# Score products of 128 columns, a doubled key rest, split compressed keys and separate pools for small tiles in a two-layer attention trunk

## The chip, the cores and the metric

The kernel runs on one core of one Trainium2 chip. The metric is device time in microseconds (us) of one execution; lower is better. The engines named below are PE (TensorE: matrix products and the loads of their stationary operand, shown apart as PEld), DVE (VectorE), ACT (ScalarE), POOL (GpSimd) and SP (SyncE, which here only issues DMA transfers).

## The reference

A sequence of 1024 tokens of width 1024 goes through two decoder layers in float32. Layer 0 has sparse attention with three branches, layer 1 has dilated sliding-window attention, and each is followed by a SwiGLU. There are 16 heads of width 64 in 4 groups (`g`), and the 4 heads of a group share keys and values. Cut to what the change touches:

```
def nsa_attention(h, ...):                      # layer 0
    q, kc, vc, ks, vs, kwn, vwn, gl = split(h @ w_in)
    k_cmp = gelu(blocks(kc) @ w1) @ w2          # 63 compressed keys per group
    s = q @ k_cmp.T * dh**-0.5 + bias           # (1) compressed branch
    p_cmp = softmax(s)
    imp = sum_heads(p_cmp) @ overlap            # importance of 16 blocks of 64 keys
    sel = top_k(imp + forced, 8)                # 8 of 16 blocks per query and group
    o_sel = softmax(q @ ks.T + bias, keys of sel)  @ vs     # (2) selected blocks, causal
    o_win = softmax(q @ kwn.T + bias, 0 <= i - j <= 255) @ vwn   # (3) window
    return (g0 * o_cmp + g1 * o_sel + g2 * o_win) @ w_out

def dilated_attention(h, ...):                  # layer 1: three (window, dilation) groups,
    for window, dilation in ((128, 1), (512, 4), (2048, 16)):    # merged by their denominators
        o, lse = banded attention over every dilation-th key
```

## The kernel before

Activations lie transposed, so that heads stand on partitions. To keep float32 accuracy with the fast product type, an operand is split into a high part and a rest (`split`: ACT writes the high part, DVE the difference). A query tile `Q` holds the high part of 64 dimensions in partitions 0 to 63 and its rest in partitions 64 to 127. A key tile whose high part (or rest) is stored twice, in both halves of the partitions (`load_k` does that with two DMAs), therefore gives the product with the whole query in one pass. A score is the sum of two products: query times key high part (first line, L676) and query times key rest (second line, L677).

**Layer 0's attention** (called A here) works on 32 units, `(g, t)`: 4 groups by 8 blocks of 128 queries. `jobs` yields for each unit two window jobs (`dense_job` with `br` 2, one for each pair of heads `hp`), the compressed job of the next unit (`cmp_job`) and two jobs over the selected keys (`dense_job` with `br` 1). Block `t` sees the keys of blocks 0 to `t`, so a selected job has `n = 128 * (t + 1)` columns. From `t` = 4 on, the choice of blocks is applied in the product itself: the second product takes its query from `QM`, with 16 mask rows below the 64 rows of the high part, and the key rest with the block indicator `bS` in rows 64 to 79, 80 rows in all. For `t` below 4 all blocks are chosen; there the second product uses the 64 rows of the key rest alone. A job's scores go through a fused add-bias-and-minimum on DVE (L679), exp on ACT (L685), the scaling by 1/sum and gate on POOL (L689), and then, in `back` and two jobs later, through PE transposes (L276), a split on ACT (L139) and DVE (L140), and the products with the values (L297 to L299).

Products narrower than 256 columns are done 256 wide before the change, as in `w, rw = max(hi - lo, 256), hi - lo`, and the surplus columns are never read. The compressed scores (L601) take the 64-column key tile `kc` in plain float32; the built program has 128 such products, and the profile shows two hardware instructions for each.

**Layer 1's attention** (called B) has for each group eight `wide_job` positions `r` (dilation 4, L1490, and dilation 16, L1495, side by side in one bank) and eight `near_job` positions `t` (dilation 1, L1510), two jobs each. `unit` does for them what `dense_job` does (DVE L1454, ACT L1459). `load_first` loads the first group's operands in three pieces, since their producers finish just before. The row minima and sums go into the small tiles `st12` and `st0`.

**What sets the order.** The order on each engine's queue is set when the program is built, by a scheduler that runs the traced program through a timing model of its own; each engine then executes its queue strictly in order. Tiles come from pools, which are laid on two stacks of on-chip memory. A new pool may lie on memory that an earlier stage still uses; the first instruction that writes a tile there waits for the last users of the old one. DMAs with `nc.sync` are all in SP's one queue, those with `nc.gpsimd` in POOL's. Before the change, the small tiles of a few columns (`m`, `sm`, `cm`, `st12` and others) are in the same pool `wk` as the large ones. In A, the key rest and all else that does not fit earlier lies in pool `aB` (`kB`), which comes after the projections.

Of the kernel before, what the change touches and what calls it, by code (L numbers as in the profile page):

```python
# [24 lines left out]
G = 4  # L25
# [66 lines left out]
def trunk(ctx, tc, I, out):  # L92
# [244 lines left out]
    kc = ares.tile([128, G, DH], F32, name="kc")  # L337
# [5 lines left out]
    with ExitStack() as c:  # L343
# [51 lines left out]
        def compress(i, kc2, weights):  # L395
            pe, w1, w2 = (("a_pe_k", "a_w1_k", "a_w2_k"), ("a_pe_v", "a_w1_v", "a_w2_v"))[i]
            pet = cp.tile([128, 16], F32, name="pet", bufs=2)
            nc.gpsimd.dma_start(pet, I[pe][0].rearrange("(i two) d -> (two d) i", two=2))
            w2t = cp.tile([128, 2, 2, 64], F32, name="w2t", bufs=1)
            for u in range(2):  # L400
                nc.gpsimd.dma_start(w2t[:, :, u, :], I[w2][0].rearrange("(a p) d -> p a d", p=128))
            ps = [bank(f"cmp{hd}")[:, :256] for hd in range(2)]
            for q in range(4):
                wh, wl = weights.load(I[w1][0][q * 512:(q + 1) * 512, :], 4, 256)
                for r in range(4):
                    ch = 4 * q + r
# [12 lines left out]
            yield  # L419
            ps2 = bank("cmp0")[:, :256]  # L420
            if i == 0:
                hh = cp.tile([128, 2, 256], F32R, name="hh")
                hl = cp.tile([128, 2, 256], F32R, name="hl")
                split(hh, hl, hid)
                w2h = cp.tile([128, 2, 128], F32R, name="w2h")
                w2l = cp.tile([128, 2, 128], F32R, name="w2l")
                split(w2h, w2l, w2t[:].rearrange("p a u d -> p a (u d)"))
                for hd in range(2):
                    mm3(ps2, (w2h[:, hd], w2l[:, hd]), (hh[:, hd], hl[:, hd]), hd == 0, hd == 1)
                nc.vector.tensor_copy(kc, ps2.rearrange("p (g n) -> p g n", n=DH))  # L430
# [87 lines left out]
    with ExitStack() as c:  # L518
# [11 lines left out]
        rC = Ring("C", [128, 4, 63], F32, [(kA1, 1), (kB, 1)])  # L530

        rM = Ring("QM", [128, 4, 512], F32R, [(kB, 1)])
        force = kB.tile([128, NT, 16], F32, name="force")
        nc.sync.dma_start(force, I["force"])
        crow = kB.tile([128, 1], F32, name="crow")
# [12 lines left out]
        def load_bias(g, a, heads=range(4)):  # L548
# [4 lines left out]
            for hh in heads:  # L553
# [3 lines left out]
                if a == 1:  # L557
# [4 lines left out]
                    nc.gpsimd.tensor_copy(C[:, hh, 31:], every)  # L562
# [4 lines left out]
        def load_ks(g):  # L567
            K = grp["K", g] = [rKs.tile() for _ in range(2)]
            load_k(K[0], kS[0, g, 0])
            nc.sync.dma_start(f32(K[1][0:64]), kS[0, g, 1])  # L570
            nc.sync.dma_start(f32(K[1][64:80]), bS)

# [21 lines left out]
        def cmp_job(g, t):  # L594
# [3 lines left out]
            for hp in range(2):  # L598
                ps = bank("s")[:].rearrange("p (e n) -> p e n", e=2)
                for e in range(2):  # L600
                    nc.tensor.matmul(ps[:, e, :DH], f32(query(g, t, 2 * hp + e)), kc[:, g, :], start=True, stop=True)  # L601
                    psv.append(ps[:, e, :])
# [3 lines left out]
            mx = wk.tile([128, 4], F32, name="cm", bufs=3)  # L606
            dn = wk.tile([128, 4], F32, name="cd", bufs=3)
# [11 lines left out]
            dg = wk.tile([128, 4], F32, name="dg", bufs=3)  # L619
            nc.vector.tensor_mul(dg, dn, gt(g, t, 0, 0, 4))  # L620
            if t >= 4:
                pn = wk.tile([128, 4, 64], F32, name="pn", bufs=2)
                nc.gpsimd.tensor_mul(pn[:, :, :nv], pv, dn[:].unsqueeze(2).to_broadcast([128, 4, nv]))
            nc.gpsimd.tensor_mul(pv, pv, dg[:].unsqueeze(2).to_broadcast([128, 4, nv]))
            if t >= 4:
                a4 = wk.tile([128, 68], F32, name="a4", bufs=2)
# [3 lines left out]
                sc = wk.tile([128, 16], F32, name="sc", bufs=2)  # L630
# [3 lines left out]
                m8 = wk.tile([128, 8], F32, name="m8", bufs=2)  # L634
                nc.vector.max(out=m8, in_=sc)
                s2_ = wk.tile([128, 16], F32, name="s2", bufs=2)
                nc.vector.match_replace(out=s2_, in_to_replace=m8, in_values=sc, imm_value=-3e38)
                mk = wk.tile([128, 16], F32, name="mk", bufs=2)
# [13 lines left out]
        def dense_job(g, t, br, hp):  # L652
# [5 lines left out]
            mm = wk.tile([128, 2], F32, name="m", bufs=8)  # L658
            sm = wk.tile([128, 2], F32, name="sm", bufs=8)
            masked = br == 1 and t >= 4  # L660
            kh, kl = grp["K", g] if br == 1 else grp["KW", g, t // 4]
            skip = 256 if br == 2 and t >= 4 else 0
            cuts = [(0, n - 512, 0), (n - 512, n, 1)] if n > 512 else [(0, n, 1)]
            mp = wk.tile([128, 2, 2], F32, name="mp", bufs=4) if len(cuts) == 2 else None
            for e in range(2):
                hh = 2 * hp + e
                q = query(g, t, hh)
                for i, (lo, hi, a) in enumerate(cuts):
                    bias = grp["T", g, a, hh] if br == 1 else grp["TW", g, hh]
                    ps = bank("s")  # L670
                    w, rw = max(hi - lo, 256), hi - lo
                    ks = slice(k0 * 128 - skip + lo, k0 * 128 - skip + lo + w)

                    nr = 128 if br == 2 else 80 if masked else 64
# [34 lines left out]
        def jobs():  # L709
# [4 lines left out]
            load_ks(0)  # L714
            load_v(0, 0, 0)
            yield lambda: cmp_job(*units[0])
            for i, u in enumerate(units):
# [7 lines left out]
                elif g + 1 < G:  # L725
# [4 lines left out]
                    elif t == 4:  # L730
                        load_q(g + 1, 0)
                    elif t == 6:
# [640 lines left out]
    with ExitStack() as c:  # L1373
        wk = pool(c, "bw")
        bB = pool(c, "bB")
        c.push(open_banks(("s",), ("pt",), ("o",)))
# [15 lines left out]
        def load_first():  # L1392
# [4 lines left out]
            for lo, hi in ((0, 256), (256, 512), (512, 1024)):  # L1397
                for i in (1, 2):
# [5 lines left out]
                    ks = slice(2 * lo, 2 * hi) if i == 1 else slice(lo + 128 * (lo > 0), min(hi + 128, S))  # L1404
# [78 lines left out]
        def wide_job(g, r, hp):  # L1483
            (Q1, K1, V1), (Q2, K2, V2) = grp[1, g], grp[2, g]

            def score(ps, hh):
# [5 lines left out]
                w = min(256, S - r * 128)  # L1492
                with after(prev):
                    for z in range(2):
                        nc.tensor.matmul(ps[:, 256:256 + w], Q2[hh][:, qs], K2[z][:, r * 128:r * 128 + w],  # L1495
                                         start=z == 0, stop=z == 1)
# [6 lines left out]
        def near_job(g, t, hp):  # L1503
# [4 lines left out]
            def score(ps, hh):  # L1508
                for z in range(2):
                    nc.tensor.matmul(ps[:, :256], Q0[hh][:, t * 128:(t + 1) * 128],  # L1510
                                     K0[z][:, k0 * 128:k0 * 128 + 256], start=z == 0, stop=z == 1)
# [5 lines left out]
        def merge(g):  # L1517
# [14 lines left out]
            s12 = wk.tile([128, NT, 8], F32, name="s12", bufs=2)  # L1532
# [3 lines left out]
            for hf in range(2):  # L1536
                yield
                cc = wk.tile([128, 4, 8], F32, name="cc", bufs=2)
                mx = wk.tile([128, 4, 4], F32, name="mx", bufs=2)
# [35 lines left out]
        def jobs():  # L1575
# [9 lines left out]
            for g in range(G):  # L1585
                grp["st", g] = (wk.tile([128, NT, 8], F32, name="st12", bufs=2),
                                wk.tile([128, NT, 8], F32, name="st0", bufs=2),
# [77 lines left out]
```

## Time and profile before

| | |
|---|---|
| runs before | 3013.38, 3020.68, 3022.80 us; median 3020.68 us |
| profiled execution | 3014.07 us |
| its span, first to last instruction | 3012.3 us (1.8 us lie around it) |
| mean granted PE clock | 0.984 |
| busy share of the span | PE 95%, PEld 79%, DVE 80%, ACT 53%, POOL 54% |
| A, first compressed score (L601) to last value product (L299) | 286.57 to 746.00 us |
| B, first wide score (L1490) to last product with the values merged (L1571) | 1910.24 to 2230.39 us |

The three runs differ by 0.3%. The profiled execution is 6.6 us below their median. In the profile's rows a name such as `s<-K,Q` is the tile written and the tiles read, with buffer numbers left out; `64*128 64x256` is a product whose stationary operand has 64 rows and 128 columns and whose moving operand has 64 rows and 256 columns. The times of matrix products overlap, because their ends are modelled: the pace of PE is read from the distance of starts, and best from the starts of the weight loads.

### The profile page before, as it was taken

What the parts mean: (1) busy time and instruction counts of PE and PEld (TensorE: products, weight loads), DVE (VectorE), ACT (ScalarE), POOL (GpSimd) and SP (SyncE); (2) the same over time, 40 slices, a digit from 0 to 9 for tenths busy, and PEclk for the clock granted to TensorE, in tenths of its full rate; (3) what the DMA queues carried; (4) which work ended last, traced back from release to release, by engine and by line L of the source; (5) the groups of instructions that cost most, each with busy time, mean ns of one, the idle gap of its engine ahead of it and who ended that gap; (6) DMA issues with size and microseconds to landing.
All of it is one profiled execution on the core that took longest, in us unless ns stands there. A gap on an engine that the chain in (4) does not pass through costs nothing.

```text
span 3012.3 us, 44147 instructions
## 1 busy us (share of the span) xinstructions
PE 2869.0 (95%) x14670; PEld 2378.2 (79%) x14670; DVE 2405.6 (80%) x4832; ACT 1600.7 (53%) x3596; POOL 1640.1 (54%) x1751
## 2 busy tenths in 40 slices
PE   7999999999889999999999999899988999999997
PEld 6988888888667878888777788788866778888886
DVE  4432888988988898898875677588899788889887
ACT  5432888887363333333364444689964533333334
POOL 2134666666766555555556787333347655555551
PEclk9999999999999999999999999999999999999999
DMA  6765032121212223222124555866520212111111
GB/s 171 221 193 167 24 105 79 33 60 58 73 51 65 64 63 78 67 58 72 56 94 143 157 164 149 267 199 183 147 95 25 63 49 63 53 53 57 56 46 74
DMA packets 266196, 293.43 MB, mean 97 GB/s; under 512 B 17971, under 2 KB 209347, under 8 KB 265968
## 3 DMA queue, kind: packets, MB, share of 16 engines
q1 hardware_dynamic: 246320, 230.45, 26.6%
q0 software_dynamic: 19648, 60.16, 6.6%
q8 instruction: 116, 1.90, 0.3%
q14 instruction: 112, 0.92, 0.1%
HBM read 227.44 MB, written 78.81 MB: 102 GB/s over the span
## 4 chain that ended last, share of the span: by engine, by line
PE 61%; DVE 22%; ACT 6%; issue 5%; DMA 3%; POOL 2%; SPq 1%; DVEq 0%; ACTq 0%; POOLq 0%
DVE pl L763 7%; PE ux L166 5%; DVE xr L821 5%; PE ux L167 5%; PE ux L168 4%; PE pt L276 4%; PE uy L166 4%; PE uy L167 4%; PE uy L168 4%; PE dx L167 3%; PE mm L166 3%; PE dx L168 3%; PE mm L167 3%; PE mm L168 2%; PE dr L166 2%
## 5 line engine op out<-in xcount | busy, mean ns | idle before, releaser
L763 DVE TENSOR_TENSOR pl<-oT,ph 128x512 fp32r<-128x512 f32 x315 | 333.7, 1079 | 40.8 <-ACT ph L762 34.6
L762 ACT ACTIVATE ph<-oT 128x512 fp32r<-128x512 f32 x329 | 198.8, 626 | 222.3 <-PE ux L167 58.5
L276 PE MATMUL pt<-ident,P 128*128 128x128 f32 x1536 | 244.5, 278 | 10.9 <-ACT P L1459 2.7
L763 DVE TENSOR_TENSOR pl<-oTb,ph 128x512 fp32r<-128x512 f32 x229 | 228.1, 1021 | 24.0 <-ACT ph L762 23.9
L762 ACT ACTIVATE ph<-oTb 128x512 fp32r<-128x512 f32 x239 | 143.1, 625 | 185.4 <-PE ux L167 51.4
L821 DVE TENSOR_TENSOR xr<-xr,dr 128x512 f32<-128x512 f32 x336 | 214.4, 678 | 28.2 <-PE dr L168 28.1
L140 DVE TENSOR_TENSOR tl<-pt,th 128x512 fp32r<-128x512 f32 (+1 forms) x320 | 206.9, 651 | 30.8 <-ACT th L139 28.7
L821 DVE TENSOR_TENSOR xr<-xr,dx 128x512 f32<-128x512 f32 x352 | 220.1, 676 | 2.9 <-PE dx L168 2.2
L167 PE MATMUL dx<-pl,ph 128*128 128x512 f32 x512 | 203.2, 401 | 9.7 <-DVE pl L763 8.6
L689 POOL TENSOR_SCALAR P<-P,sm,gates 128x384 f32<-128x384 f32 (+7 forms) x256 | 182.5, 724 | 54.1 <-DVE sm L687 48.2
L276 PEld LDWEIGHTS pt<-ident,P 128*128 128x128 f32 x1536 | 179.6, 142 | 29.9 <-ACT P L1459 6.7
L168 PE MATMUL dx<-ph,pl 128*128 128x512 f32 x512 | 199.9, 397 | 0.3 <-DVE pl L763 0.3
L139 ACT ACTIVATE th<-pt 128x512 fp32r<-128x512 f32 (+1 forms) x320 | 176.8, 563 | 41.1 <-PE pt L276 35.2
L685 ACT ACTIVATE P<-P,m 128x384 f32<-128x384 f32 (+7 forms) x256 | 170.8, 669 | 16.2 <-DVE m L683 8.2
L1082 POOL TENSOR_TENSOR oT<-oT,gffn 128x512 f32<-128x512 f32 x92 | 108.2, 1183 | 128.7 <-DMA oT<-in_ffn_w_up_dram 112.4
L166 PE MATMUL dx<-ph 128*128 128x512 f32 x512 | 157.3, 398 | 8.4 <-DVE xr L821 3.3
L1082 POOL TENSOR_TENSOR oTb<-oTb,gffn 128x512 f32<-128x512 f32 x92 | 106.1, 1160 | 92.6 <-DMA oTb<-in_ffn_w_up_dram 83.1
L299 PE MATMUL o<-tl,V 128*128 128x256 f32 x540 | 147.6, 298 | 8.4 <-POOL tl L292 4.4
L298 PE MATMUL o<-th,V 128*128 128x256 f32 x540 | 149.6, 294 | 2.4 <-ACT th L139 1.3
L291 POOL TENSOR_SCALAR th<-traw 128x128 fp32r<-128x128 f32 (+1 forms) x112 | 74.8, 671 | 126.9 <-ACT traw L290 46.3
L1459 ACT ACTIVATE P<-P,st 128x384 f32<-128x384 f32 (+2 forms) x256 | 139.5, 547 | 7.7 <-PE pt L1570 4.1
L167 PEld LDWEIGHTS dx<-pl,ph 128*128 128x128 f32 x512 | 97.5, 190 | 40.7 <-DVE pl L763 21.1
(617 smaller groups left out, 9547.6 us busy)
## 6 DMA issues: line engine op xcount, KB each, us to landing
qB<-xr POOLq DMA_DIRECT2D x96, 256.0 KB, 4.9
oT<-in_ffn_w_up_dram SPq DMA_DIRECT2D x92, 256.0 KB, 3.0
oTb<-in_ffn_w_up_dram SPq DMA_DIRECT2D x92, 256.0 KB, 3.0
Q<-qB SPq DMA_DIRECT2D x40, 512.0 KB, 8.2
wd<-in_ffn_w_down_dram SPq DMA_DIRECT2D x66, 256.0 KB, 2.7
oT<-in_b_w_q_dram SPq DMA_DIRECT2D x48, 256.0 KB, 3.4
K<-kBs SPq DMA_DIRECT2D x40, 256.0 KB, 10.3
wraw<-in_a_w_in_dram SPq DMA_DIRECT2D x18, 512.0 KB, 5.0
```

What stands on the lines that cost most here:

```text
L139: nc.scalar.activation(H_, src, AF.Copy)
L140: nc.vector.tensor_sub(L_, src, f32(H_))
L166: nc.tensor.matmul(ps, lh, rh, start=first, stop=False, skip_group_check=bool(shared))
L167: nc.tensor.matmul(ps, lh, rl, start=False, stop=False, skip_group_check=bool(shared))
L168: return nc.tensor.matmul(ps, ll, rh, start=False, stop=last, skip_group_check=bool(shared))
L276: nc.tensor.transpose(ps[:, i * 128:(i + 1) * 128], b, ident)
L685: nc.scalar.activation(P[:, e, :n], P[:, e, :n], AF.Exp, bias=mm[:, e:e + 1], scale=-1.0, accum_out=sm[:, e:e + 1])
L689: nc.gpsimd.tensor_scalar(P[:, e, :n], P[:, e, :n], sm[:, e:e + 1], gt(g, t, br, 2 * hp + e, 1), op0=OP.mult, op1=OP.mult)
L762: nc.scalar.activation(h, src, AF.Copy)
L763: (eng or nc.vector).tensor_sub(l, src, f32(h))
L821: nc.vector.tensor_add(xs, xs, banks[t])
L1082: nc.gpsimd.tensor_mul(v, v, gains[:, k:k + 4].unsqueeze(2).to_broadcast([128, 4, 128]))
```

## The change

Five edits, all in the two attentions:

- Score products are as wide as their scores: 128 columns where 256 were computed. In the built program 352 products become 128 wide: 96 in A, 256 in B (224 of `wide_job`'s dilation 16, 32 of `near_job` at `t` = 0).
- For `t` below 4, the second selected product no longer uses 64 rows: a new tile `KD` of 512 columns holds the key rest in both halves of the partitions, loaded by `load_kd` with two DMAs per group, and the product has 128 rows. There are 64 of these products. The mathematical sum gains the small product of both rests.
- The compressed keys are split into two tiles (`kch`, `kcl`), and each of the 128 products becomes two of the fast type.
- Small tiles move into pools of their own (`as` in A, `bs` in B), opened after the large ones, `crow` among them; `pn` has one buffer instead of two; `C` is 64 wide.
- `load_first` loads the dilation-16 keys in pieces of 256, 256 and 512 columns instead of 384, 256 and 384.

```diff
-    kc = ares.tile([128, G, DH], F32, name="kc")
+    kc = [ares.tile([128, G, DH], F32R, name=f"kc{z}") for z in "hl"]
...
-                nc.vector.tensor_copy(kc, ps2.rearrange("p (g n) -> p g n", n=DH))
+                split(*kc, ps2.rearrange("p (g n) -> p g n", n=DH))
...
-        rC = Ring("C", [128, 4, 63], F32, [(kA1, 1), (kB, 1)])
-
+        rC = Ring("C", [128, 4, 64], F32, [(kA1, 1), (kB, 1)])
+
+        rKd = Ring("KD", half, F32R, [(kB, 1)])
...
-        crow = kB.tile([128, 1], F32, name="crow")
+        ws = pool(c, "as")
+        crow = ws.tile([128, 1], F32, name="crow")
...
+        def load_kd(g):
+            t = grp["KD", g] = rKd.tile()
+            load_k(t, kS[0, g, 1][:, 0:512])
...
-                    nc.tensor.matmul(ps[:, e, :DH], f32(query(g, t, 2 * hp + e)), kc[:, g, :], start=True, stop=True)
+                    for z in range(2):
+                        nc.tensor.matmul(ps[:, e, :DH], query(g, t, 2 * hp + e), kc[z][:, g, :], start=z == 0,
+                                         stop=z == 1)
...
-                pn = wk.tile([128, 4, 64], F32, name="pn", bufs=2)
+                pn = wk.tile([128, 4, 64], F32, name="pn", bufs=1)
...
-            mm = wk.tile([128, 2], F32, name="m", bufs=8)
-            sm = wk.tile([128, 2], F32, name="sm", bufs=8)
+            mm = ws.tile([128, 2], F32, name="m", bufs=8)
+            sm = ws.tile([128, 2], F32, name="sm", bufs=8)
             masked = br == 1 and t >= 4
             kh, kl = grp["K", g] if br == 1 else grp["KW", g, t // 4]
+            if br == 1 and not masked:
+                kl = grp["KD", g]
...
-                    w, rw = max(hi - lo, 256), hi - lo
+                    w = rw = hi - lo
...
-                    nr = 128 if br == 2 else 80 if masked else 64
+                    nr = 80 if masked else 128
...
             load_ks(0)
+            load_kd(0)
...
                         load_q(g + 1, 0)
+                        load_kd(g + 1)
...
+        ws = pool(c, "bs")
...
-                    ks = slice(2 * lo, 2 * hi) if i == 1 else slice(lo + 128 * (lo > 0), min(hi + 128, S))
+                    ks = slice(2 * lo, 2 * hi) if i == 1 else slice(lo, hi)
...
-                w = min(256, S - r * 128)
                 with after(prev):
                     for z in range(2):
-                        nc.tensor.matmul(ps[:, 256:256 + w], Q2[hh][:, qs], K2[z][:, r * 128:r * 128 + w],
-                                         start=z == 0, stop=z == 1)
+                        nc.tensor.matmul(ps[:, 256:384], Q2[hh][:, qs], K2[z][:, qs], start=z == 0, stop=z == 1)
...
-                    nc.tensor.matmul(ps[:, :256], Q0[hh][:, t * 128:(t + 1) * 128],
-                                     K0[z][:, k0 * 128:k0 * 128 + 256], start=z == 0, stop=z == 1)
+                    nc.tensor.matmul(ps[:, :n], Q0[hh][:, t * 128:(t + 1) * 128],
+                                     K0[z][:, k0 * 128:k0 * 128 + n], start=z == 0, stop=z == 1)
...
-                grp["st", g] = (wk.tile([128, NT, 8], F32, name="st12", bufs=2),
-                                wk.tile([128, NT, 8], F32, name="st0", bufs=2),
+                grp["st", g] = (ws.tile([128, NT, 8], F32, name="st12", bufs=2),
+                                ws.tile([128, NT, 8], F32, name="st0", bufs=2),
                                 wk.tile([128, 2, S], F32, name="o12", bufs=2))
```

The edit changes the scheduler's input, and the order of A and B differs in many places; outside them it does not differ but for a few rows. Three places matter below. The first is PE's queue in A, third group, `t` = 2. `K_4608` and `K_4609` are the key's high part and rest, `VW` and `KW` belong to the window. Before:

```order
L648 MATMUL o<-th,vc 128x512
L649 MATMUL o<-tl,vc 128x512
L298 MATMUL o<-th,V_4614 128x256
L676 MATMUL s<-K_4608,Q_5145 128x384
L677 MATMUL s<-K_4609,Q_5145 128x384
L676 MATMUL s<-K_4608,Q_5147 128x384
L677 MATMUL s<-K_4609,Q_5147 128x384
L299 MATMUL o<-tl,V_4614 128x256
```

After:

```order
L297 MATMUL o<-traw,VW_5721 128x256
L276 MATMUL pt<-ident,P_6553 128x128 x4
L686 MATMUL s<-K_4659,Q_5208 128x384
L687 MATMUL s<-KD_5212,Q_5208 128x384
L298 MATMUL o<-th,V_4665 128x256
L686 MATMUL s<-K_4659,Q_5210 128x384
L687 MATMUL s<-KD_5212,Q_5210 128x384
L299 MATMUL o<-tl,V_4665 128x256
```

The pairs of score products stand as they did, close together among value products; the second of a pair now reads `KD`.

The second place is SP's queue where A's last loads before its first unit stand, with the waits that the built program gives them (DMAHW is an earlier DMA on a queue of SP, DMASW one of POOL). Before:

```order
L581 DMA V_2601<-vS 128x4x128 [waits DMAHW4_49]
L534 DMA force<-in_force_dram 128x128 [waits DMAHW5_49]
L536 DMA crow<-in_cmprow_dram 128x1 [waits DMAHW6_49]
L546 DMA QM_2585<-qS 64x4x512 [waits DMAHW7_49]
L555 DMA T_2729<-sA 128x512 [waits DMAHW0_49]
```

After:

```order
L587 DMA V_2613<-vS 128x4x128 [waits DMAHW4_49]
L538 DMA crow<-in_cmprow_dram 128x1 [waits DMAHW5_49,PE_49]
L535 DMA force<-in_force_dram 128x128 [waits DMAHW6_49]
L268 DMA KD_2551<-kS 64x512 [waits DMAHW7_49]
L269 DMA KD_2551<-kS 64x512 [waits DMAHW0_49]
L548 DMA QM_2597<-qS 64x4x512 [waits DMAHW1_49]
```

`crow` now stands first and waits for PE: its new place is memory that holds the projections' last operand `hH7` until then. `force`, both loads of `KD` and `QM` stand behind it.

The third place is DVE's queue at the start of B, where the last results of the projections (`xr`, which POOL's DMAs store to `qB`) are followed by the first scores. Before:

```order
L1022 TENSOR_TENSOR c_19386<-c_19386,dr1_19357 128x512 [waits Activation_49]
L143 SCALAR_TENSOR_TENSOR xr_9957<-uy_19248,xr_9957 128x512 [waits Activation_49]
L1038 TENSOR_TENSOR d1_19351<-d1_19351,dr1_19357 128x512 [waits PE_49]
L143 SCALAR_TENSOR_TENSOR xr_9957<-d1_19351,xr_9957 128x512 [waits Activation_49]
L1454 ISA P_19567,st12_19564<-s_19568,T120_19477 128x384 [waits DMAHW4_49,DMAHW3_49,PE_49]
L1454 ISA st12_19564 128x1
```

After:

```order
L1050 TENSOR_TENSOR d1_19497<-d1_19497,dr1_19503 128x512 [waits PE_49]
L143 SCALAR_TENSOR_TENSOR xr_10103<-d1_19497,xr_10103 128x512 [waits Activation_49]
L1394 CAST rowsel_19620<-rows_19618 128x512 [waits DMAHW3_49]
L1467 ISA P_19716,st12_19713<-s_19717,T120_19626 128x384 [waits DMASW4_49,DMASW3_49,DMASW5_49,DMASW2_49,DMASW6_49,DMASW1_49,DMASW7_49,DMASW0_49,DMAHW4_49,DVE_49,PE_49]
L1467 ISA st12_19713 128x1
```

The first score instruction now waits for POOL's DMAs too, since pool `bs` lies on the end of `xr`.

More of the change, by code (lines that the diff above doesn't have):

```diff
@@ L561, in load_bias @@
                     grp["TW", g, hh] = w_
-                    nc.gpsimd.tensor_copy(C[:, hh, 31:], every)
+                    nc.gpsimd.tensor_copy(C[:, hh, 31:63], every)
                 else:
@@ L605, in cmp_job @@
             nc.gpsimd.memset(pc[:, :, nv:64], 0.0)
-            mx = wk.tile([128, 4], F32, name="cm", bufs=3)
-            dn = wk.tile([128, 4], F32, name="cd", bufs=3)
+            mx = ws.tile([128, 4], F32, name="cm", bufs=3)
+            dn = ws.tile([128, 4], F32, name="cd", bufs=3)
             for hh in range(4):
@@ L618, in cmp_job @@
                 nc.vector.tensor_scalar(dn, dn, crow, None, op0=OP.mult)
-            dg = wk.tile([128, 4], F32, name="dg", bufs=3)
+            dg = ws.tile([128, 4], F32, name="dg", bufs=3)
             nc.vector.tensor_mul(dg, dn, gt(g, t, 0, 0, 4))
             if t >= 4:
-                pn = wk.tile([128, 4, 64], F32, name="pn", bufs=2)
+                pn = wk.tile([128, 4, 64], F32, name="pn", bufs=1)
                 nc.gpsimd.tensor_mul(pn[:, :, :nv], pv, dn[:].unsqueeze(2).to_broadcast([128, 4, nv]))
@@ L625, in cmp_job @@
             if t >= 4:
-                a4 = wk.tile([128, 68], F32, name="a4", bufs=2)
+                a4 = ws.tile([128, 68], F32, name="a4", bufs=2)
                 nc.gpsimd.memset(a4, 0.0)
@@ L629, in cmp_job @@
                                         op=OP.add)
-                sc = wk.tile([128, 16], F32, name="sc", bufs=2)
+                sc = ws.tile([128, 16], F32, name="sc", bufs=2)
                 nc.vector.tensor_reduce(sc, a4[:, 1:65].rearrange("p (j i) -> p j i", i=4), axis=AX.X, op=OP.add)
@@ L633, in cmp_job @@
                 nc.vector.tensor_add(sc, sc, force[:, t, :])
-                m8 = wk.tile([128, 8], F32, name="m8", bufs=2)
+                m8 = ws.tile([128, 8], F32, name="m8", bufs=2)
                 nc.vector.max(out=m8, in_=sc)
-                s2_ = wk.tile([128, 16], F32, name="s2", bufs=2)
+                s2_ = ws.tile([128, 16], F32, name="s2", bufs=2)
                 nc.vector.match_replace(out=s2_, in_to_replace=m8, in_values=sc, imm_value=-3e38)
-                mk = wk.tile([128, 16], F32, name="mk", bufs=2)
+                mk = ws.tile([128, 16], F32, name="mk", bufs=2)
                 nc.vector.tensor_scalar(mk, s2_, -2e38, BIG, op0=OP.is_gt, op1=OP.mult)
@@ L657, in dense_job @@
             P = wk.tile([128, 2, 1024 if br == 1 else 384], F32, name=f"P{br}", bufs=4)
-            mm = wk.tile([128, 2], F32, name="m", bufs=8)
-            sm = wk.tile([128, 2], F32, name="sm", bufs=8)
+            mm = ws.tile([128, 2], F32, name="m", bufs=8)
+            sm = ws.tile([128, 2], F32, name="sm", bufs=8)
             masked = br == 1 and t >= 4
             kh, kl = grp["K", g] if br == 1 else grp["KW", g, t // 4]
+            if br == 1 and not masked:
+                kl = grp["KD", g]
             skip = 256 if br == 2 and t >= 4 else 0
             cuts = [(0, n - 512, 0), (n - 512, n, 1)] if n > 512 else [(0, n, 1)]
-            mp = wk.tile([128, 2, 2], F32, name="mp", bufs=4) if len(cuts) == 2 else None
+            mp = ws.tile([128, 2, 2], F32, name="mp", bufs=4) if len(cuts) == 2 else None
             for e in range(2):
@@ L1531, in merge @@
                 nc.tensor.transpose(px[:, t * 8:(t + 1) * 8], rows[:, t * 128:(t + 1) * 128], ident[:8, :8])
-            s12 = wk.tile([128, NT, 8], F32, name="s12", bufs=2)
+            s12 = ws.tile([128, NT, 8], F32, name="s12", bufs=2)
             nc.vector.tensor_copy(s12, px[:, :64].rearrange("p (t c) -> p t c", c=8))
@@ L1537, in merge @@
                 yield
-                cc = wk.tile([128, 4, 8], F32, name="cc", bufs=2)
-                mx = wk.tile([128, 4, 4], F32, name="mx", bufs=2)
+                cc = ws.tile([128, 4, 8], F32, name="cc", bufs=2)
+                mx = ws.tile([128, 4, 4], F32, name="mx", bufs=2)
                 ts = slice(4 * hf, 4 * hf + 4)
```

## Prediction

> **What bounds the kernel now.** I read first the busy shares of the engines (the page's first part), then the table of windows for one head group of each attention, then the chain that ended last.
>
> ```profile
> PE 2869.0 (95%) x14670; PEld 2378.2 (79%) x14670; DVE 2405.6 (80%) x4832; ACT 1600.7 (53%) x3596; POOL 1640.1 (54%) x1751
> PE 61%; DVE 22%; ACT 6%; issue 5%; DMA 3%; POOL 2%; SPq 1%; DVEq 0%; ACTq 0%; POOLq 0%
> 444.00:505.00 61.00, 58.30 (x394) 50.78 (x393) 56.68 (x225) 50.58 (x133) 43.11 (x71) 1.00 0.21 64
> 505.00:556.00 51.00, 50.99 (x344) 43.74 (x343) 41.20 (x177) 45.63 (x153) 31.99 (x55) 1.00 0.32 82
> 505.00:536.00 31.00, 30.99 (x225) 27.70 (x224) 23.58 (x101) 26.29 (x92) 19.55 (x34) 1.00 0.36 83
> 536.00:556.00 20.00, 20.00 (x120) 16.05 (x120) 17.62 (x77) 19.34 (x63) 12.44 (x21) 1.00 0.27 80
> 2035.00:2110.00 75.00, 70.88 (x542) 64.57 (x543) 67.68 (x231) 67.86 (x206) 23.28 (x40) 1.00 0.65 181
> ```
>
> The windows give length, then busy time of PE, PEld, DVE, ACT and POOL, then the granted clock. A's third group shows two halves: in its masked half (444 to 505 us) PE idles 2.7 us and DVE is nearly as full; in the half without mask (505 to 556 us, `t` of 0 to 3 with their neighbours) PE idles 0.01 us of 51. So a PE saving in the second half shortens it, until ACT (45.63 us) becomes the bound. In a group of B PE has 4.1 us idle in 75, DVE 7.3 and ACT 7.1: three engines close together. The edit touches only A and B; the order elsewhere is unchanged.
>
> **The 64 products of 64 rows.** All stand in the half without mask. The next rows are that half's groups for L677, and the starts of weight loads around two pairs of scores, then a pair of the same width whose two operands both have 128 rows.
>
> ```profile
> L677 PE MATMUL s<-K,Q 64*128 64x256 f32 x8 | 3.0, 381 | 0.0
> L677 PE MATMUL s<-K,Q 64*128 64x512 f32 x4 | 2.0, 498 | 0.0
> L677 PE MATMUL s<-K,Q 64*128 64x384 f32 x4 | 1.7, 437 | 0.0
> ...
> 538.16 0.18 PEld L677 LDWEIGHTS s<-K,Q 64*128 64x128 f32 x1 [0.19 <-issue]
> 538.52 0.19 PEld L676 LDWEIGHTS s<-K,Q 128*128 128x128 f32 x1 [0.18 <-DVE tl L140]
> 538.90 0.18 PEld L677 LDWEIGHTS s<-K,Q 64*128 64x128 f32 x1 [0.19 <-issue]
> 539.26 0.19 PEld L299 LDWEIGHTS o<-tl,V 128*128 128x128 f32 x1 [0.18 <-DVE m L679]
> ...
> 567.37 0.34 PE L676 MATMUL s<-KW,Q 128*128 128x384 f32 x1
> 567.54 0.34 PE L677 MATMUL s<-KW,Q 128*128 128x384 f32 x1
> 567.72 0.40 PE L648 MATMUL o<-th,vc 128*128 128x512 f32 x1
> ```
>
> The 64-row load begins only some 0.18 us after its engine came free, and so does the 128-row load behind it: a pair takes 538.90 - 538.16 = 0.74 us. The pair with 128 rows takes 567.72 - 567.37 = 0.35 us. A 64-row product thus costs 0.39 us more than a 128-row one. 8 + 4 + 4 = 16 of them make 6.2 us of the half's 51; four groups, 25 us. `KD` removes it, if all of it goes with the row count: the moving columns are the same.
>
> How much PE then really gives back, per group: PE needs 50.99 - 6.2 = 44.8 us, less than ACT's 45.63. In the last 20 us, 536 to 556, ACT was busy 19.34 of 20.00 us, 97%, which I take as what it can keep up: 45.63 / 0.97 = 47.0 us. The half becomes 47.0 instead of 51.0, a gain of 4.0 us; what is late next is the exp and the split (ACT L685, L139), and behind them DVE L140. Groups two to four: 12 us. The first group's half is the stretch in which A starts:
>
> ```profile
> 285.00:320.00 35.00, 33.06 (x167) 26.90 (x166) 21.65 (x121) 26.70 (x100) 17.75 (x43) 0.80 0.30 75
> ```
>
> PE idles 1.9 us there and the granted clock is 0.80. Bounds for this group are 0 (its pace is the start's loads) and 6.2; I take the middle, 3.
>
> **The narrower products (352) and the split compressed keys (128).** The starts of weight loads in B's second group, and those of the compressed scores in A:
>
> ```profile
> 2101.81 0.30 PEld L1490 LDWEIGHTS s<-K,Q 128*128 128x128 f32 x2
> 2102.04 0.31 PEld L1495 LDWEIGHTS s<-K,Q 128*128 128x128 f32 x2
> 2102.30 0.53 PEld L276 LDWEIGHTS pt<-ident,P 128*128 128x128 f32 x5
> ...
> 568.64 0.53 PEld L601 LDWEIGHTS s<-kc,Q 128*128 128x128 f32 x4
> 569.10 0.19 PEld L299 LDWEIGHTS o<-tl,VW 128*128 128x128 f32 x1
> ...
> 2101.59 0.33 PE L1495 MATMUL s<-K,Q 128*128 128x128 f32 x2
> 2101.76 0.28 PE L299 MATMUL o<-tl,V 128*128 128x128 f32 x1
> ```
>
> Two 256-wide products of L1490 take 2102.04 - 2101.81 = 0.23 us, 0.115 each. The two of L1495, which at the last position are 128 wide already, take 0.26, 0.13 each; products of only 64 columns (L601) take (569.10 - 568.64) / 4 = 0.115. The pace is the load of the stationary operand, whatever the columns. So narrowing gains about nothing per product: the lower end is 0; the upper end is 0.03 (the L1495 pair by its matmul starts, 0.17 / 2 = 0.085, against 0.115), that is 352 x 0.03 = 10.6 us. I take 0.01 each, 3.5 us of PE time, because three of these four readings stand at 0.115 or above: 1 in A, below what I can separate, and 2.6 in B, of which PE's cover by DVE and ACT leaves 1. The Trainium skill ("TensorE: Matmul & The Clock Gate", section "LDWEIGHTS (loading the stationary operand)") gives 107 ns for loading 128 columns, against which the rows here show 115. [...]
>
> The split: before, the profile has two hardware loads for each of the 128 compressed products (the four rows above are two products), after it has two fast products: 256 loads either way, 0 us. Bounds: -7.7 if each of the 256 came down by 0.03, +7.7 if up. The extra ACT operation for `kcl` runs once, in the projections. One buffer for `pn` puts POOL's next write behind DVE's read, which is done well before: 0.
>
> **The new waits.** At A's start `crow` waits for PE's last projection product; `force`, the two `KD` loads and `QM` are queued behind it on SP. Issue rows of before, then the PE rows that set the new times, then landing times of the nearest loads:
>
> ```profile
> 232.86 0.34 SPq L534 DMA_DIRECT2D force<-in_force_dram  x1
> 234.46 0.33 SPq L536 DMA_DIRECT2D crow<-in_cmprow_dram  x1
> ...
> 286.34 0.39 PE L168 MATMUL mm<-hH,wl 128*128 128x512 f32 x1
> ...
> 290.88 0.38 PE L677 MATMUL s<-K,Q 64*128 64x256 f32 x1
> ...
> qS<-sth POOLq DMA_DIRECT2D x2, 128.0 KB, 2.4
> KW<-kS SPq DMA_DIRECT2D x4, 128.0 KB, 3.8
> ```
>
> That product ends at 286.34 + 0.39 = 286.73 instead of `crow` going out at 234.46. With `force` ahead and about 0.34 us per issue on SP, `KD` (128 KB a half) goes out near 288.5 and lands 2.4 to 3.8 us later, 290.9 to 292.3. The first product that needs it stood at 290.88, and the new order puts some 25 more PE instructions ahead of it, so most of this is covered. `QM` is needed only from `t` = 4. Cost 0 to 3.4 us (the late DVE score after a late `crow`, or the wait for `KD`); I take 1, since the earliest row of need is nearly at the landing. The later `KD` loads come at `t` = 4, when the products of `t` = 3 are past: 0.
>
> A, together: 12 + 3 - 1 = 14 us less.
>
> At B's start the first score on DVE now waits for the stores of `xr` that POOL issues, since the minima's tiles lie on that memory:
>
> ```profile
> 1912.09 2.08 POOL L1289 DMA_DIRECT2D qB<-xr  x4 [1.39 <-ACT xr L142]
> 1912.44 0.55 DVE L1454 CUSTOM_DVE_ANT_0 P<-s,T 128x384 f32<-128x384 f32 x1
> 1913.05 0.50 PE L1490 MATMUL s<-K,Q 128*128 128x256 f32 x2 [1.22 <-DVE st L1454]
> 1918.77 0.48 PE L1490 MATMUL s<-K,Q 128*128 128x256 f32 x2 [1.97 <-DMA K<-kBs]
> 1921.19 0.68 PE L1490 MATMUL s<-K,Q 128*128 128x256 f32 x2 [1.60 <-DMA K<-kBs]
> 1954.00 0.47 PE L299 MATMUL o<-tl,V 128*128 128x128 f32 x1 [4.45 <-POOL tl L292]
> ...
> qB<-xr POOLq DMA_DIRECT2D x16, 256.0 KB, 5.7
> ```
>
> The last four stores go out from 1912.09 to 1914.17; with 5.7 us to landing they end near 1919.9 instead of DVE starting at 1912.44: up to 7.4 us. Behind DVE's wait stand all its scores; PE gets a few banks of scores ahead and then waits, and with it ACT. Cover: PE idled there 1.22 + 1.97 + 1.60 us for `K` loads and 4.45 us at 1954, in sum 9.2, most of which the late start merely fills, since PE, ACT and DVE all have less than their full work until 1954. So 0 to 7.4; I take 1, nearer 0 because the cover is larger than the delay. B then: -1 + 1 = 0.
>
> **The sum.** 3014.07 (own time of the profiled execution) - 14 + 0 = 3000. Its own time is 6.6 us below the median of the runs, 3020.68. Against the median that is 3006.7; I forecast 3007 us.
>
> **The rivals.**
>
> 1. *The whole PE saving arrives.* ACT's 19.34 of 20 us hold work that can as well be done elsewhere, since the new order is free to put a job's exp and split beside the masked half, where ACT has 50.58 of 61. For: the 31 us from 505 to 536 have ACT at 26.29 only (85%). Against: the last 20. It gives 25 us and 1 to 3 from B, 3020.7 - 27 = 2994.
>
> 2. *Narrow products run at their columns' pace.* For: the L1495 pair, by matmul starts. Against: 0.115 for 64 columns. At 256 columns in 0.115 and 128 in half of it, 0.058, the gain is 352 x 0.057 = 20 us on top: 2994 - 20 = 2974 with the first rival, near 2990 where DVE and ACT bound B. [...]
>
> 3. *The gain is hidden.* The masked half has DVE at 56.68 of 61 us: units of both halves overlap in the pipeline, and what the half without mask finishes early waits for DVE and ACT work behind it. For: POOL and ACT waits are many there. Against: PE's 0.01 us idle in 51. It gives 0 to 8 us less: 3013 to 3021.
>
> 4. *Slower: the stores at B's start.* The 7.4 us of DVE's wait are paid in full, as the whole pipeline of B (PE, DVE and ACT at 90 to 95%) starts later and does not catch up, and narrowing gives 0. It decides where A's gain is less than 7.4 us; with A at 0 and the start of A at its 3.4 us, it gives 3020.7 + 10.8 = 3031. For: three engines near full in B. Against: the 9.2 us of idle time in B's first 45 us, and A's saturated stretches.
>
> That the change does not do what it says: `KD` is in the new order beside Q in 128 rows, so only the stall's cause is in doubt. If it comes from the 64 rows of the stationary operand, it goes; were it another property of these pairs (their place among value products, or the key rest's tile), the pairs would stay at 0.74 us, and the time would be that of rival 3's upper end.
>
> **How the numbers follow.** The three runs differ by 0.3%, 9 us, about what a measurement of this kernel can tell from no change. My forecast (9 to 20 us faster) has 0.50; rival 1, 0.12; rival 2, 0.02: faster in all 0.64. Rival 3, within 9 us of 3020.7, 0.27. Rival 4, 0.09. The range: from 2988 (rival 1 with 6 us more from B) to 3020, the greater part of rival 3; what is left out are rival 2, rival 4 and the end of rival 3, some 0.2.
>
> **What would show it.** In the changed trace: weight loads of the pairs with `KD` start 0.11 to 0.2 us apart with no "issue" idle; the half without mask, per group, lasts about 47 us with ACT at 97%; if it is 51 with PE at 88%, rival 3. The 128-wide products of L1503 and L1507 start their loads 0.11 us apart; at 0.06, rival 2. PE idles less than 2 us before the first `KD` product. The first DVE score of B starts up to 7 us later than the last projection, and PE's idle at 1954 shrinks by as much; if it does not shrink, rival 4. The prediction is wrong if ACT bounds the half without mask at 51 us, or if the new order of A, which differs in many places, stalls PE somewhere that neither trace of before shows.

## The result, and the profile after

The changed kernel took 3045.74 us in the median of four runs (3043.95 to 3048.88), the kernel before 3017.03 us (3012.62 to 3022.80): a ratio of 1.0095, 95% interval 1.0072 to 1.0118. It is slower, and the forecast of 3007 us was wrong in size and sign. The profiled execution of the changed kernel has a span of 3044.9 us, against 3012.3.

The loss lies in A. The windows below are A from its first compressed score to its last value product, and a whole group of it, from the second pair of scores of `t` = 2 in the third group to the same pair in the fourth (called the third group here), for the kernel before and the changed one (length; PE, PEld, DVE, ACT, POOL busy; granted clock).

```profile
286.57:746.00 459.43, 445.64 (x2929) 383.51 (x2927) 393.00 (x1595) 385.93 (x1128) 300.38 (x489) 0.98 0.21 59
535.80:647.10 111.30, 109.13 (x734) 94.21 (x733) 98.41 (x401) 95.88 (x283) 73.42 (x119) 1.00 0.19 53
```

```profile
287.44:774.30 486.86, 440.72 (x2929) 389.90 (x2927) 404.99 (x1595) 384.32 (x1128) 299.39 (x489) 0.95 0.22 60
546.90:666.20 119.30, 106.01 (x732) 92.79 (x731) 102.10 (x398) 95.34 (x281) 73.05 (x119) 1.00 0.19 52
```

A became 27.4 us longer, while the number of PE records stayed at 2929. In the third group, where both clocks are 1.00, PE's busy time fell from 109.13 to 106.01 us, half of the 6.2 us that the rows of the 64-row products promised, but PE's idle time rose from 2.2 to 13.3 us. No engine is full there: PE 89%, DVE 86%, ACT 80%. B, counted here from the start of its first wide score to the start of its last value product, went from 314.8 to 319.3 us; the runs below show that such a difference in B can't be read.

What PE waited for in that group of the changed kernel (us in total, times, longest), and then, from the timeline, one such wait on PE and POOL's rows ahead of it (`th` is the high part of a transposed window block, which POOL makes on L291 and its rest `tl` on L292):

```profile
PE o L298 <- POOL th L291: 4.3, 3, 2.3
PE o L299 <- POOL tl L292: 2.2, 3, 1.0
PE s L686 <- DVE mp L689: 2.0, 3, 1.2
PE s L686 <- DVE m L689: 1.3, 3, 0.7
PE pt L276 <- DVE tl L140: 1.0, 3, 0.5
```

```profile
619.97 0.39 PE L298 MATMUL o<-th,VW 128*128 128x256 f32 x1 [2.30 <-POOL th L291]
...
615.66 3.44 POOL L699 TENSOR_SCALAR P<-P,sm,gates 128x896 f32<-128x896 f32 x4
619.07 0.85 POOL L291 TENSOR_SCALAR th<-traw 128x256 fp32r<-128x256 f32 x1
```

PE's queue has the product with `th` at its head, and everything behind it waits; POOL makes `th` only after four scalings of 896 columns (3.44 us). There is no one big wait: the longest is 2.3 us, and the waits come from POOL, DVE and ACT.

The products with `KD` themselves are as forecast. Their weight loads in the same group:

```profile
554.55 0.19 PEld L686 LDWEIGHTS s<-K,Q 128*128 128x128 f32 x1
554.66 0.19 PEld L687 LDWEIGHTS s<-KD,Q 128*128 128x128 f32 x1
554.89 0.19 PEld L686 LDWEIGHTS s<-K,Q 128*128 128x128 f32 x1
555.12 0.19 PEld L687 LDWEIGHTS s<-KD,Q 128*128 128x128 f32 x1
```

Each starts 0.11 to 0.23 us after the one ahead, with no idle time, where it was 0.36 to 0.38 us before.

### The profile page after: what moved, and what is told of

The parts are those of the page before. It is cut to its first block, busy times and chain, and to the rows that moved or that the text cites. A ratio compares the mean times of both kernels' runs of the same rounds, so it can differ in the third digit from the quotient of the medians.

```text
span 3044.9 us, 44192 instructions
## 1 busy us (share of the span) xinstructions
PE 2866.6 (94%) x14670; PEld 2383.5 (78%) x14670; DVE 2410.0 (79%) x4832; ACT 1599.3 (53%) x3597; POOL 1639.2 (54%) x1751
## 4 chain that ended last, share of the span: by engine, by line
PE 55%; DVE 21%; ACT 9%; issue 6%; DMA 5%; POOL 3%; SPq 1%; DVEq 0%; ACTq 0%; POOLq 0%
DVE pl L775 7%; DVE xr L833 5%; PE ux L166 5%; PE ux L167 4%; PE ux L168 4%; PE pt L276 3%; PE uy L166 3%; PE uy L167 3%; PE uy L168 3%; PE mm L166 2%; PE dx L167 2%; PE mm L167 2%; PE mm L168 2%; PE dx L168 2%; PE dr L166 2%
## 5 line engine op out<-in xcount | busy, mean ns | idle before, releaser
L276 PE MATMUL pt<-ident,P 128*128 128x128 f32 x1536 | 250.5, 284 | 16.9 <-DVE tl L140 7.8
L276 PEld LDWEIGHTS pt<-ident,P 128*128 128x128 f32 x1536 | 181.5, 145 | 37.5 <-DVE tl L140 10.0
L695 ACT ACTIVATE P<-P,m 128x384 f32<-128x384 f32 (+7 forms) x256 | 170.5, 669 | 13.3 <-DVE m L693 9.0
L291 POOL TENSOR_SCALAR th<-traw 128x128 fp32r<-128x128 f32 (+1 forms) x112 | 74.8, 670 | 130.2 <-ACT traw L290 48.0
L1467 DVE CUSTOM_DVE_ANT_0 P<-s,T 128x384 f32<-128x384 f32 (+2 forms) x256 | 115.2, 474 | 22.5 <-PE pt L276 8.7
```

The source lines that it names most:

```text
L276: nc.tensor.transpose(ps[:, i * 128:(i + 1) * 128], b, ident)
L695: nc.scalar.activation(P[:, e, :n], P[:, e, :n], AF.Exp, bias=mm[:, e:e + 1], scale=-1.0, accum_out=sm[:, e:e + 1])
```

## The experiments

Lengths of A are those of the window from first compressed score to last value product; PE idle is that length less PE's busy time. Both, and B, are read from one profiled execution of each kernel; the expectations end A at the start of that product, some 0.3 us earlier. Each ratio is to runs of the kernel before in the same round of measurements (medians 3014.82 to 3017.03 us), so it is not always the quotient of the medians shown.

| run | edits | order of the queues | median us | ratio to before (95%) | A us | PE idle in A us | B us |
|---|---|---|---|---|---|---|---|
| before | none | own | 3017.03 | 1 | 459.4 | 13.8 | 314.8 |
| changed | all | own | 3045.74 | 1.0095 (1.0072-1.0118) | 486.9 | 46.1 | 319.3 |
| e1_kd | `KD` | own | 3001.95 | 0.9961 (0.9943-0.998) | 446.0 | 22.8 | 314.2 |
| e2_narrow | narrow | own | 3025.55 | 1.0031 (1.0017-1.0046) | 465.8 | 20.5 | 315.3 |
| e3_kc | split `kc` | own | 3031.58 | 1.0065 (1.0042-1.0088) | 474.7 | 23.5 | 319.3 |
| e4_pools | pools | own | 3022.24 | 1.0019 (1.0004-1.0034) | 460.0 | 16.3 | 321.1 |
| p_after_bo | all | before's | 3006.03 | 0.9964 (0.9949-0.998) | 448.7 | 21.4 | 315.9 |
| p_before_ao | none | changed's | 3055.36 | 1.0139 (1.0115-1.0163) | 491.8 | 38.0 | 317.3 |
| p_kc_bo | split `kc` | before's | 3020.24 | 1.0016 (1.0004-1.0029) | 461.0 | 14.6 | 313.3 |
| p_kd_bo | `KD` | before's | 2999.45 | 0.9952 (0.9936-0.9969) | 442.3 | 20.1 | 319.5 |
| q1_splits | all | changed's, POOL's splits moved | 3038.67 | 1.0074 (1.0053-1.0095) | 479.3 | 40.9 | 319.8 |
| q4_pe_bo | all | PE before's, others own | 3010.03 | 0.9977 (0.9955-0.9999) | 452.1 | 24.2 | 323.3 |
| q2_kdn_bo | `KD`, narrow | before's | 2999.86 | 0.9946 (0.9925-0.9967) | 444.5 | 20.9 | 317.3 |
| q3_nobs_bo | all but `bs` | before's | 2997.02 | 0.9937 (0.992-0.9953) | 442.8 | 20.7 | 316.4 |

### One edit at a time, each in the order that the scheduler gives it

Theory 1 was that the new order of the queues makes the loss; theory 2, its rival, that the pools and the single `pn` buffer do, by waits of their own. Each kernel is the one before with one part of the diff alone: `KD`; both narrowings; the split compressed keys; the pools with `pn` and `C`. Their diffs are these parts of the change's diff, word for word.

> Before with KD alone (its ring, its loads, 128 rows in the second product for t below 4). Theory 1 (the PE time is saved, but the order of the queues that comes with it leaves PE waiting for the choice of blocks, and the clock drops after such waits): pairs of a KD product in 0.35 us, PE's busy time in A some 25 us less, and A no shorter or up to 25 us longer than the 459 us of before. Theory 2 (the small pools and the single pn buffer make the waits): A 12 to 20 us shorter, run 3000 to 3008 us.

> Before with the narrow products alone (A and B). Theory 1: PE time as before within 4 us, but the order changes in A and B, so either may move by up to 15 us in either direction. Theory 2: A and B as before within 4 us, run 3010 to 3020 us.

> Before with the split compressed keys alone. Theory 1: PE time the same (256 loads either way), A within 5 us of 459 where the order is little changed, more where it changes. Theory 2: as before within 4 us.

> Before with the pools alone (as, bs, one buffer for pn, C 64 wide, crow in as). Theory 1: A as before within 5 us, B up to 7 us longer by the first score's wait for the stores of xr. Theory 2: A 28 us longer and B 3 to 7 us longer, as in the changed kernel: run 3040 to 3048 us.

`KD` alone did what the prediction's sum had for it: A 13.4 us shorter, the ratio 0.9961. Theory 1 had expected A no shorter and missed here; theory 2's figure was met. The pools alone left A as it was (460.0), where theory 2 asked for 28 us more, so theory 2 fell. The split keys alone, priced at nothing in the prediction, made A 15.2 us longer; the narrow products 6.3, and their run, 3025.55 us, lies above theory 2's 3010 to 3020. The four changes in A's length add up to +8.7 us, against +27.4 for all the edits together, so the loss is not a sum of what single edits cost by themselves. The windows of A for `KD` alone and for the split keys alone:

```profile
287.00:733.00 446.00, 423.24 (x2929) 377.05 (x2927) 392.04 (x1595) 384.38 (x1129) 301.53 (x489) 0.99 0.23 64
```

```profile
286.54:761.20 474.66, 451.21 (x2929) 384.05 (x2927) 396.49 (x1595) 384.77 (x1128) 299.52 (x489) 0.98 0.21 58
```

With `KD` PE's busy time in A is 445.64 - 423.24 = 22.4 us less. With the split keys it is 5.6 us more and the idle time 9.7 us more, at the same number of products. Whether that is the edit's own work or the order that came with it, these runs can't tell.

### Work and order apart

The order of every engine's queue can be held. After the program is traced, each instruction gets an edge to the one that shall stand ahead of it on its engine, which asks for the issue order alone and adds no wait:

```diff
         trunk(tc, aps, o)
+        hold_order(tc, nc)
...
+    for e in ORDER:
+        queue = [traced[e][k] for k in ORDER[e]]
+        for a, b in zip(queue, queue[1:]):
+            tc.add_manual_dep(b, a.name, mybir.DependencyInfo(mybir.DependencyClass.NoSync, ...))
```

`ORDER` lists, for each engine, the instructions of this kernel in the order in which their counterparts stand in the other kernel. The `KD` loads and the one more operation that splits the compressed keys have no counterpart in before and stand where the scheduler puts them. In the traces of the four kernels below, all other rows of PE's loads, DVE, ACT and POOL in A stand in the order asked for, without an exception.

Theory 2 is from here on that the edits' own work and waits cost the time.

> The changed kernel, all five edits, with each engine's queue held to the order of before (the eight KD loads stand where the scheduler puts them). Theory 1 (the loss is the order that the scheduler makes for the edited program, not the edits' own work): the pairs with KD save their 22 us of PE time, A 440 to 448 us instead of 486.6, B 315 to 322, run 2995 to 3010 us. Theory 2 (the edits' work and waits themselves, the split compressed keys above all, cost the time): A 470 us or more, run 3030 to 3046 us.

> The kernel before, none of the edits, with each engine's queue held to the order of the changed kernel. Theory 1: A as long as in the changed kernel or longer, since the 64-row products keep their 22 us: 480 to 500 us instead of 459, run 3035 to 3060 us. Theory 2: A within 5 us of 459, run 3012 to 3024 us.

> The split compressed keys alone, held to the order of before. By itself, with its own order, this edit made A 474.4 us and the run 3031.6. Theory 1: A 457 to 462 us, run 3012 to 3022 us. Theory 2: A 470 us or more, run 3028 us or more.

> KD alone, held to the order of before. With its own order it made A 445.7 us and the run 3002. Theory 1: A 440 to 450 us, run 2996 to 3006 us; if it is longer than 450, the order of before holds back a part of the saving. Theory 2 says the same.

The windows of A for all edits in before's order, with its third group, and for no edit in the changed kernel's order:

```profile
288.05:736.74 448.69, 427.27 (x2929) 384.24 (x2927) 392.56 (x1595) 384.33 (x1128) 301.19 (x489) 0.97 0.23 65
531.30:639.50 108.20, 104.11 (x734) 93.52 (x733) 98.16 (x399) 95.41 (x283) 73.55 (x119) 1.00 0.21 57
```

```profile
287.04:778.80 491.76, 453.75 (x2928) 385.67 (x2927) 406.60 (x1595) 385.12 (x1128) 300.49 (x489) 0.98 0.20 56
```

| A, us | before's order | changed kernel's order |
|---|---|---|
| no edit | 459.4 | 491.8 |
| all edits | 448.7 | 486.9 |

Theory 1 holds, with A 0.7 us above the end of its range for the changed kernel in before's order. The order costs 32.3 us without any edit and 38.2 us with all of them; the edits themselves save 10.7 us in the one order and 4.9 in the other. Without edits, at a mean clock of 0.98 in both orders, 24.2 of the 32.3 us are more idle time of PE and 8.1 a longer busy time; with them it is 24.7 and 13.5, the last at clocks of 0.97 and 0.95. The split keys in before's order leave A at 461.0 us and PE's busy time at 446.3 against 445.6: as forecast they cost next to nothing, and the 15 us that they made alone were their order (13.7 of it goes when the order is held). The third group shows it most plainly: with the same edits and a clock of 1.00 PE is busy 104.11 us in the one order and 106.01 in the other, and the group lasts 108.20 or 119.30. Most of the difference is idle time, 4.1 against 13.3 us.

PE's waits in the third group with all edits in before's order:

```profile
PE s L686 <- DVE m L689: 1.2, 2, 0.8
PE pt L649 <- DVE mk L647: 0.6, 1, 0.6
PE o L299 <- DVE tl L140: 0.5, 2, 0.3
PE pt L276 <- DVE cd L623: 0.4, 1, 0.4
PE o L298 <- POOL th L291: 0.3, 1, 0.3
```

The 4.3 and 2.2 us for POOL's splits are 0.3 and none here.

The half without mask, for which the prediction had worked out 47.0 us, shows what bounds it once the order is kept. The windows are the third group's, between the same instructions, before and with `KD` alone in before's order:

```profile
504.99:556.10 51.11, 51.10 (x345) 43.85 (x343) 41.31 (x177) 45.74 (x154) 32.10 (x55) 1.00 0.32 82
```

```profile
494.31:541.58 47.27, 45.97 (x345) 43.23 (x343) 41.59 (x177) 43.65 (x144) 31.75 (x55) 1.00 0.36 93
```

The length came as forecast, but PE is still the fullest engine, at 97%, and ACT has 92%, with ten instructions fewer than before. PE's busy time fell by 5.1 us, not by 6.2.

### Which queue

In `q1_splits` the table `ORDER` is the changed kernel's own but for POOL's rows; `q4_pe_bo` holds one engine:

```diff
-    for e in ORDER:
+    for e in ("PE",):
```

> The changed kernel in its own order, with one thing moved: in POOL's queue each of the 48 splits of a window block (L291, L292) stands where its input was ready in the trace of the changed kernel (L292 right behind its L291), ahead of up to seven rows that it stood behind. All other queues keep the changed kernel's order. PE idled 10.8 and 7.4 us ahead of the products with these splits. If their place in POOL's queue makes the loss (theory A): these two waits shrink to under 6 us in sum and A falls from 486.6 to 465 to 475 us, run 3025 to 3035. If it is PE's order, which asks for them too early (theory B): the waits shrink by less than half, or come back ahead of other products, and A stays above 478 us.

> The changed kernel with PE's queue alone held to the order of before; the other queues are the scheduler's own, made for that PE order. Theory A: A stays above 465 us, since POOL's queue is again the scheduler's. Theory B: A falls to 445 to 455 us, as with all queues held (448.7).

The groups of PE's transposes and of its products with POOL's splits, over all of A, first in the changed kernel, then with the splits moved (the last part is the idle time ahead of them):

```profile
L276 PE MATMUL pt<-ident,P 128*128 128x128 f32 x912 | 147.3, 283 | 11.4 <-DVE tl L140 7.8 <-ACT traw L282 1.8 <-ACT QM L650 0.8
...
L299 PE MATMUL o<-tl,VW 128*128 128x256 f32 x108 | 34.6, 331 | 7.4 <-POOL tl L292 7.2
L298 PE MATMUL o<-th,VW 128*128 128x256 f32 x108 | 34.4, 321 | 10.8 <-POOL th L291 10.7
```

```profile
L276 PE MATMUL pt<-ident,P 128*128 128x128 f32 x912 | 147.0, 283 | 13.2 <-DVE tl L140 7.4 <-ACT traw L282 2.3 <-DVE cd L623 1.5
L298 PE MATMUL o<-th,VW 128*128 128x256 f32 x108 | 34.2, 320 | 3.1 <-POOL th L291 3.1
L299 PE MATMUL o<-tl,VW 128*128 128x256 f32 x108 | 33.9, 326 | 1.2 <-POOL tl L292 1.2
```

Moving the splits took these two waits from 18.2 to 4.3 us, but in the profiled execution A fell by only 7.5 us and PE's idle time from 46.1 to 40.9: the rest came back ahead of other products (the transposes of L276, for one, from 11.4 to 13.2 us). Theory A asked for 465 to 475 us, theory B for over 478, and A was 479.3. But this kernel ran only twice, the profiled execution took 3043.53 us, and the other, of 3033.81 us, lies in theory A's range; so these two runs do not decide.

PE's queue alone in before's order brought A to 452.1 us, 34.8 of the 38.2 us, with the other queues ordered by the scheduler around it. That PE's order alone makes the loss does not follow: given PE's order, the scheduler also put 1375 of DVE's 1595 instructions in A, 1094 of ACT's 1128 and 448 of POOL's 489 at the places that they have with all queues held to before's order; in the changed kernel it is 387, 647 and 244. So before's order on PE is enough to bring back most of the whole order and of the time. Which queue and which of its many places weigh how much is not shown, nor why the scheduler, whose plan goes by a timing model of its own, makes this order of the edited program.

### What is left of the narrow products and of the wait at B's start

`q2_kdn_bo` has the parts of the diff for `KD` and for the narrow products; `q3_nobs_bo` has all but this, and leaves B's other small tiles in the large pool likewise:

```diff
-        ws = pool(c, "bs")
...
-                grp["st", g] = (ws.tile([128, NT, 8], F32, name="st12", bufs=2),
-                                ws.tile([128, NT, 8], F32, name="st0", bufs=2),
+                grp["st", g] = (wk.tile([128, NT, 8], F32, name="st12", bufs=2),
+                                wk.tile([128, NT, 8], F32, name="st0", bufs=2),
```

> KD and the narrow products, without the split compressed keys and the pools, all queues in the order of before. With KD alone in this order A was 442.3 and B 319.5 (with more low clock than before's 314.8) and the run 2999.5. If narrowing saves some 4 us of PE time in B as the busy time of the changed kernel in before's order says (284.8 against 288.8): A 441 to 444, B 310 to 316, run 2994 to 3000. If the load of the stationary operand sets the pace whatever the columns: within 1 us of KD alone.

> The changed kernel without pool bs (st12, st0 and the other small tiles of B back in the large pool), all queues in the order of before. In the changed kernel the first score on DVE came 11.1 us after the first product of B, before 2.2. If that wait is paid: the distance falls to about 2 us and B from 315.9 to 309 to 312, run 2999 to 3003 against 3006. If idle time further on takes it: B within 2 us of 315.9.

`KD` with the narrow products took 2999.86 us, `KD` alone 2999.45: narrowing gives nothing that these runs can tell, as the unchanged pace of the weight loads in the prediction says. B is 317.3 us against 319.5, but B scatters as much without any edit: `KD` alone in before's order has B's work and order as before, and its B took 319.5 us against 314.8, at a granted clock of 0.97 against 0.98.

The wait at B's start is real. The first products of B and the first score on DVE in the changed kernel:

```profile
1936.00 0.88 PE L1503 MATMUL s<-K,Q 128*128 128x256 f32 x6
1947.73 0.79 PE L1503 MATMUL s<-K,Q 128*128 128x256 f32 x2 [10.23 <-DVE st L1467]
...
1947.11 0.56 DVE L1467 CUSTOM_DVE_ANT_0 P<-s,T 128x384 f32<-128x384 f32 x1 [8.49 <-DMA qB<-xr]
```

The distance from B's first product to its first score on DVE is 11.1 us, before it is 2.2. With all edits in before's order it is 12.0; without the pool `bs` in that order it is 2.2 again, yet B took 316.4 us against 315.9: later idle time takes the wait in, or it is lost in B's scatter. The run is 9 us shorter, 2997.02 against 3006.03, but 5.9 us of the profiled difference lie in A, which that edit doesn't touch, and A's mean clock was 0.99 against 0.97. This kernel, `KD` with the narrow products, split keys and pool `as` in before's order, is the fastest of all that ran, and faster than both kernels; it can't be told apart from `KD` alone in that order.

## Why the prediction was wrong, point by point

- **The bound.** Right that PE's work was the bound in the half without mask, and that less of it shortens A once the order is kept. Wrong in what bounds it then: the forecast 47.0 us rested on ACT at 97%, and with `KD` alone in before's order the half took 47.3 us with PE at 97% and ACT at 92%. That the length agrees is luck in part. (The window of 444 to 505 us that the prediction calls the third group's masked half belongs to the second group; its readings stand.)
- **The 64-row products.** Right. Forecast 25 us of PE time, measured 22.4 with its own order and 23.4 with before's; forecast 15 us (12 + 3) off A, measured 13.4 with its own order and 17.1 with before's. The Trainium skill ("TensorEngine Tiling (Array Packing)", section "Key Properties") says that a change of tiling mode drains the engine; the trace agrees with it, in that the load of a 64-row product and the load behind it were late by 0.18 to 0.19 us in the rows shown, and with 128 rows are not. That 64 rows mean another mode is not shown by a run; 80 rows have no such delay, their loads start 0.11 us after the load ahead (median of 128 in the kernel before; 0.37 for the 64).
- **The narrow products and the split keys.** Their work was priced rightly as far as single profiled executions can tell, 1 us less and 0 us in A: with the order held, the split keys made A 1.5 us longer, and narrowing made it 2.2 us longer (442.3 to 444.5).
- **A's start.** The path came as worked out: `KD` went out at 288.49 us, forecast near 288.5. The forecast cost of 1 us can't be read apart from the order.
- **B's start.** The wait was there and longer than its upper end (8.9 us later, against 7.4). Taking 1 us for its cost was nearer than rival 4's full price. Of the cover, the 1.22 us are no wait for `K`, as the prediction's text has it, but for DVE, as its row says.
- **The step that failed** is the sum for A: it added the terms of the edits and put nothing down for the new order of the queues. The change part showed the pairs at one place where they stood as before and went on from there; that the order of A differs in many places stood only among the things that would make the prediction wrong. That term was the largest of all: +38 us, against -11 for the edits together. No rival had it either. What failed is thus the step from PE work saved to time saved: with all edits, PE is idle 24.7 us longer in A in the changed kernel's order than in before's. Rival 4 named the right side by another mechanism, which was measured and not paid.

## What to carry to other kernels

Where a scheduler sets the queues' order, an edit is two changes, its work and a new order, and here the second was three times the first with the opposite sign. Hold the order of the old kernel with issue-order edges and time the edit so; then time the old kernel in the new order. When engines are all 80 to 90% busy and none is full, look at what the head of PE's queue waits for: here a sum of many waits of at most 2.3 us came from the order, and not from a full engine.

## What the hardware showed beside this

PE's granted clock halved with only short idle pieces ahead of it. Four windows of the changed kernel's second group:

```profile
444.00:448.00 4.00, 2.80 (x19) 2.11 (x17) 4.00 (x25) 3.95 (x16) 4.00 (x6) 1.00 0.09 25
448.00:452.00 4.00, 3.28 (x10) 2.08 (x8) 3.44 (x10) 3.21 (x10) 4.00 (x9) 0.54 0.00 0
452.00:456.00 4.00, 3.88 (x14) 3.08 (x14) 3.83 (x13) 0.65 (x2) 1.99 (x4) 0.50 0.00 0
456.00:460.00 4.00, 4.00 (x25) 3.91 (x24) 2.66 (x12) 1.72 (x4) 0.00 (x0) 0.68 0.00 0
```

And the longest idle piece in the first of them:

```profile
447.34 0.88 PE L276 MATMUL pt<-ident,P 128*128 128x128 f32 x6 [0.61 <-ACT traw L282]
```

PE was idle for 1.2 of 4 us, in pieces of 0.61 us at most, and then ran at half clock for some 10 us, although it was 82 to 100% busy. Waits of the same kind in the third group, with one of 2.3 us at 619.97, left the clock at 1.00. The Trainium skill ("TensorE: Matmul & The Clock Gate", section "HAM oscillation — how this bites in real kernels") gives as its abstract rule no idle gaps of over about 3.4 us; this trace shows the half clock without such a gap. Whether the waits bring the half clock is not shown. It is not the main cost here: without any edit the mean clock in A was 0.98 in both orders, and the changed kernel's order still took 32.3 us more. With all edits it was 0.95 in the changed kernel's order and 0.97 in before's; an estimate from these clocks and the lengths of A (5% of 486.9 us against 3% of 448.7) leaves some 11 of the 38.2 us to the clock.
